# Down-projection of seven of eight feed-forward blocks as seven products of halves

## The chip, the cores and the metric

The kernel runs on one core of one Trainium2 chip. The metric is the device time of one execution in microseconds; lower is better. The core's engines are PE (matmul, with its weight loads listed as PEld), DVE (vector), ACT (scalar), POOL (GpSimd) and SP, which here issues the DMAs. Each engine works through its own queue in order, and semaphores tie the queues together.

## What is computed

One inference step of a two-layer streaming encoder for 1024 prompt frames and 64 sample frames, together T = 1088 columns. The mixing part of a layer (three kinds of attention) isn't touched. The feed-forward part is

```python
D_MODEL = 1024
DEPTH = 2
D_FF = 4 * D_MODEL
...
def _ffn(h, w_up, w_down):
    u = jax.nn.relu(jnp.einsum('bsd,df->bsf', h, w_up))
    return jnp.einsum('bsf,fd->bsd', u * u, w_down)
...
        xp = xp + _ffn(rmsnorm(xp, g_ffn[l]), w_up[l], w_down[l])
        xs = xs + _ffn(rmsnorm(xs, g_ffn[l]), w_up[l], w_down[l])
```

All data are float32. A product is made of three matmuls: each operand is split into a rounded high part and a low remainder (float32r), and high by high, high by low and low by high are summed in PSUM.

## The kernel before

Activations lie transposed, features on the 128 partitions and the T columns in three chunks (`CH`: 384, 384 and 320). The residual `x` is eight tiles of 1088 columns in SBUF. `phase3` runs the feed-forward part of a layer as eight blocks of 512 inner features, one after the other (`ffn_block`, b = 0 to 7).

A block has an up half and a down half. The up half takes four weight tiles (f = 0 to 3) of 128 by 1024: `weight` loads one by DMA, ACT casts it to the high part (L121), DVE subtracts to get the low part (L106). `mm3w` (L977, L979) then makes 8 k-tiles by 3 terms by 3 chunks = 72 matmuls. Each chunk's sum leaves PSUM through `evacuate`: DVE applies relu and the norm factor (L989), ACT squares it into the high part of `U[f]` (L990), POOL squares it in full precision, DVE subtracts the two for the low part.

The down half takes four more weight tiles. Each gives two of the eight output tiles, 4 k-tiles by 3 terms by 3 chunks = 36 matmuls for each, and DVE adds the three PSUM chunks to `x` (L106). So each half has 288 matmuls. There are 8 PSUM buffers (`mm`), 4 buffers for split weights (`wp`), 4 for `U`. The last block (b = 7) runs its last six output tiles chunk by chunk, beside the next layer's norm; this stays as it is.

The order on each engine isn't written out: a scheduler with a time model of its own sets it from the dependencies when the kernel is built.

## Time and profile before

| | us |
|---|---|
| median of 3 runs (lowest to highest) | 2835.04 (2831.56 to 2840.52) |
| the profiled execution's own time | 2833.1 |
| its span | 2831.2 |
| busy of the span: PE, DVE, ACT, POOL | 2748.0, 1458.3, 1066.8, 447.3 |

The span counts from the first to the last instruction of the profiled execution. Busy time on PE is not PE at its peak, since matmuls are pipelined: a record lasts longer than the distance to the next one's start, and it is this distance that counts. The two feed-forward parts are the stretches in which PE is full and DVE, ACT and POOL are low.

### The profile page before, as it was taken

The page shows a single profiled execution, that of the slowest core. Times are in us where ns is not written, and L with a number is a line of the kernel's source. Part 1 is how long each engine was busy: PE and PEld are TensorE (multiplying, and loading weights), DVE is VectorE, ACT ScalarE, POOL GpSimd, SP SyncE. Part 2 cuts the span into 40 slices and gives each one's busy share as a digit, 9 for nine tenths or more (in the row PEclk, how much of TensorE's full clock was granted, in tenths as well). Part 3 has the DMA queues.
Part 4 walks back from the last instruction along what each step waited for, and adds up shares of the span by engine and source line. Part 5 has one row for each costly group of instructions (what it writes and reads, how often), then busy time and mean ns, then how long its engine had stood idle before and what let it go on. Part 6 is the DMA issues. An engine that isn't in the chain of part 4 may idle for free. (4 is left out here: it accounts for less than half of the span.)

```text
span 2831.2 us, 44128 instructions
## 1 busy us (share of the span) xinstructions
PE 2748.0 (97%) x16918; PEld 2651.0 (94%) x16918; DVE 1458.3 (52%) x2968; ACT 1066.8 (38%) x2289; POOL 447.3 (16%) x588
## 2 busy tenths in 40 slices
PE   7999999999999999999999999999999999999997
PEld 6998888899999999999999888888999999999997
DVE  6677676665333333333647786675733333333335
ACT  5666577543111111111437665774521111111113
POOL 1112233201001100110111122431011001101112
PEclk9999999999999999999999999999999999999998
DMA  6657754551111111111265667445311111111111
GB/s 205 203 172 207 237 133 124 158 184 60 41 43 44 46 45 45 46 45 45 75 218 177 190 183 226 139 146 168 129 48 42 44 45 45 45 45 46 45 38 64
DMA packets 211811, 300.34 MB, mean 106 GB/s; under 512 B 34832, under 2 KB 180880, under 8 KB 211600
## 3 DMA queue, kind: packets, MB, share of 16 engines
q1 hardware_dynamic: 211600, 297.51, 34.0%
q8 instruction: 134, 2.20, 0.3%
q14 instruction: 77, 0.63, 0.1%
HBM read 205.72 MB, written 91.72 MB: 105 GB/s over the span
## 5 line engine op out<-in xcount | busy, mean ns | idle before, releaser
L121 ACT CAST w<-wraw 128x1024 fp32r<-128x1024 f32 (+1 forms) x190 | 198.0, 1043 | 1051.2 <-PE mm L979 986.4
L977 PE MATMUL mm<-h,w 128*128 128x384 f32 (+1 forms) x2880 | 550.5, 325 | 0.0
L977 PE MATMUL mm<-u,w 128*128 128x384 f32 (+1 forms) x2784 | 545.0, 328 | 0.0
L977 PEld LDWEIGHTS mm<-h,w 128*128 128x128 f32 x2880 | 500.8, 188 | 0.0
L977 PEld LDWEIGHTS mm<-u,w 128*128 128x128 f32 x2784 | 481.3, 188 | 0.0
L106 DVE TENSOR_TENSOR x<-mm,x 128x384 f32<-128x384 f32 (+1 forms) x432 | 210.3, 530 | 412.2 <-PE mm L979 398.7
L106 POOL TENSOR_TENSOR u<-t 128x384 f32<-128x384 f32 (+1 forms) x192 | 152.0, 791 | 1295.6 <-DVE t L989 1295.6
L979 PE MATMUL mm<-h,w 128*128 128x384 f32 (+1 forms) x1440 | 321.8, 332 | 0.0
L979 PE MATMUL mm<-u,w 128*128 128x384 f32 (+1 forms) x1392 | 311.9, 327 | 0.0
L989 DVE SCALAR_TENSOR_TENSOR t<-mm,r 128x384 f32<-128x384 f32 (+1 forms) x192 | 102.0, 531 | 363.0 <-PE mm L979 362.7
L106 DVE TENSOR_TENSOR w<-wraw,w 128x1024 fp32r<-128x1024 f32 (+2 forms) x244 | 240.1, 1002 | 91.6 <-ACT w L121 90.4
L213 PE MATMUL mm<-h,w 128*128 128x384 f32 (+1 forms) x720 | 242.1, 336 | 15.1 <-ACT w L121 12.3
L979 PEld LDWEIGHTS mm<-h,w 128*128 128x128 f32 x1440 | 241.5, 188 | 0.0
L979 PEld LDWEIGHTS mm<-u,w 128*128 128x128 f32 x1392 | 238.1, 188 | 0.0
L215 PE MATMUL mm<-h,w 128*128 128x384 f32 (+1 forms) x720 | 236.8, 329 | 0.3 <-DVE w L106 0.3
L214 PE MATMUL mm<-h,w 128*128 128x384 f32 (+1 forms) x720 | 236.5, 329 | 0.0
L990 ACT ACTIVATE u<-t 128x384 fp32r<-128x384 f32 (+1 forms) x192 | 97.1, 506 | 204.6 <-DVE t L989 204.6
L106 DVE TENSOR_TENSOR u<-u,u 128x384 fp32r<-128x384 f32 (+1 forms) x192 | 102.5, 534 | 108.6 <-POOL u L106 105.7
L213 PEld LDWEIGHTS mm<-h,w 128*128 128x128 f32 x720 | 136.5, 190 | 18.3 <-ACT w L121 12.3
L214 PEld LDWEIGHTS mm<-h,w 128*128 128x128 f32 x720 | 136.5, 190 | 1.0
L215 PEld LDWEIGHTS mm<-h,w 128*128 128x128 f32 x720 | 136.2, 189 | 0.9 <-DVE w L106 0.8
L758 POOL TENSOR_SCALAR P<-P,mx 128x640 f32<-128x640 f32 (+8 forms) x144 | 101.1, 706 | 208.9 <-DVE mx L757 141.6
(169 smaller groups left out, 4503.0 us busy)
## 6 DMA issues: line engine op xcount, KB each, us to landing
wraw<-in_w_up SPq DMA_DIRECT2D x64, 512.0 KB, 3.6
wraw<-in_w_dn SPq DMA_DIRECT2D x64, 512.0 KB, 3.5
wraw<-in_w_ft SPq DMA_DIRECT2D x24, 512.0 KB, 4.8
Q<-scr_qc SPq DMA_DIRECT2D x64, 128.0 KB, 3.2
Q<-scr_qa SPq DMA_DIRECT2D x64, 128.0 KB, 3.1
qn<-scr_qn SPq DMA_DIRECT2D x32, 256.0 KB, 3.0
Q<-scr_qr SPq DMA_DIRECT2D x64, 128.0 KB, 2.8
scr_qn<-qsp SPq DMA_DIRECT2D x16, 384.0 KB, 3.3
```

The lines of the kernel that those rows point to most:

```text
L106: (eng or self.nc.vector).tensor_tensor(out, a, b, op=op)
L121: self.nc.scalar.copy(w[:, 0], raw)
L213: nc.tensor.matmul(ps, whi(k), rhs(0, k), start=first and k == 0, stop=False)
L214: nc.tensor.matmul(ps, whi(k), rhs(1, k), start=False, stop=False)
L215: nc.tensor.matmul(ps, wlo(k), rhs(0, k), start=False, stop=last and k == nk - 1)
L758: nc.gpsimd.tensor_scalar(P, P, mx[:, 4:5], 0.0, op0=ALU.mult, op1=ALU.add)
L977: nc.tensor.matmul(ps[:, :n], whi(k), rhs(j, k, o, n), start=k == 0 and j == 0, stop=False)
L979: nc.tensor.matmul(ps[:, :n], wlo(k), rhs(0, k, o, n), start=False, stop=k == nk - 1)
L989: nc.vector.scalar_tensor_tensor(t, ps[:, :n], 0.0, rs[c][:, :n], op0=ALU.max, op1=ALU.mult)
L990: nc.scalar.activation(u[:, 0, o:o + n], t, AF.Square)
```

## The change

For blocks 0 to 6 of each layer the down half is made another way (`ffn_down`). The block's weight (512 inner features by 1024 outputs) is four quarters `A11` to `A22`, its activations four quarters `B11` to `B22` (256 features by 544 columns, `HT`). Where the plain way makes eight products of quarters, the new one makes seven products of sums and differences of quarters (Strassen's scheme in Winograd's form). A product is 4 output tiles by 2 k-tiles by 3 terms by 2 column halves of 272 (`QT`) = 48 matmuls, so the down half has 336 matmuls of 272 columns where it had 288 of 384 or 320.

The operands of each product are split anew (`split_w`, `split_u`: a cast on ACT, a subtraction on DVE, 128 by 1024 or 1088). The sums of weights are four 128 by 1024 operations on POOL, in place in the raw tiles `wd`; the sums of activations are four on DVE, in place in `U`, which is now plain float32, written by POOL's square alone. DVE adds every product's PSUM tiles to a quarter of `x` or to a new accumulator `v`. Products 1, 3 and 5 go to a second quarter too: ACT copies the PSUM tile to `tq` and POOL adds it. After block 6, DVE adds `v` to three quarters of `x`. The loads are as many bytes as before, four of 512 KB in each block.

```diff
+HT = T // 2
+QT = T // 4
...
-            up = self.pool(es, "up", 4, side="right")
+            up = self.pool(es, "up", 2, side="right")
-            np = self.pool(es, "np", 1, side="right")
+            wd = self.pool(es, "wd", 4, side="right")
-            for c in range(3):
-                list(self.prep(x, G_FFN + 8 * l, H2, c, np, sh[c]))
+            with ExitStack() as e1:
+                np = self.pool(e1, "np1", 1, side="right")
+                for c in range(3):
+                    list(self.prep(x, G_FFN + 8 * l, H2, c, np, sh[c]))
-            for b in range(7):
-                self.ffn_block(l, b, x, H2, rs, up, tp, mm, late)
+            with ExitStack() as e1:
+                v = self.pool(e1, "v", 1, side="right").tile([128, 4, HT], F32, name="v")
+                tq = self.pool(e1, "tq", 2, side="right")
+                for b in range(7):
+                    U = [up.tile([128, 2, T], F32, name="U", tag="U") for _ in range(2)]
+                    raws = [[wd.tile([128, WSLOT], F32, name="wd", tag="wd") for _ in range(2)] for _ in range(2)]
+                    self.ffn_up(l, b, H2, rs, tp, mm, late, lambda f: U[f // 2][:, f % 2])
+                    self.ffn_down(l, b, x, U, raws, up, mm, v, tq)
+                for d in range(4):
+                    for m, h in ((0, 1), (1, 0), (1, 1)):
+                        xq = x[:, 4 * m + d, HT * h:HT * h + HT]
+                        self.tt(xq, xq, v[:, d], ALU.add)
+            np = self.pool(es, "np", 1, side="right")
             if last:
                 post = lambda: [self.final(x, o, n, mm, np) for o, n in CH]
             else:
                 post = lambda: self.norm_mix(l + 1, x, mm, np, True)
-            self.ffn_block(l, 7, x, H2, rs, up, tp, mm, late, post)
+            U = [up.tile([128, 2, T], F32R, name="u", tag="uU"[f // 2]) for f in range(4)]
+            self.ffn_up(l, 7, H2, rs, tp, mm, late, lambda f: U[f], split=True)
+            self.ffn_last(l, x, U, mm, post)
 
...
-    def ffn_block(self, l, b, x, H, rs, up, tp, mm, late, post=None):
+    def ffn_up(self, l, b, H, rs, tp, mm, late, dst, split=False):
+
         nc, a = self.nc, self.a
-        U, todo = [], []
+        todo = []
 
         def evacuate(u, ps, c):
             o, n = CH[c]
             t = tp.tile([128, CW], F32, name="t", tag="t")[:, :n]
+            nc.vector.scalar_tensor_tensor(t, ps[:, :n], 0.0, rs[c][:, :n], op0=ALU.max, op1=ALU.mult)
+            if not split:
+                self.tt(u[:, o:o + n], t, t, ALU.mult, nc.gpsimd)
+                return
             u2 = tp.tile([128, CW], F32, name="u2", tag="u2")[:, :n]
-            nc.vector.scalar_tensor_tensor(t, ps[:, :n], 0.0, rs[c][:, :n], op0=ALU.max, op1=ALU.mult)
             nc.scalar.activation(u[:, 0, o:o + n], t, AF.Square)
             self.tt(u2, t, t, ALU.mult, nc.gpsimd)
             self.lo(u[:, 1, o:o + n], u2, u[:, 0, o:o + n])
...
-            U.append(up.tile([128, 2, T], F32R, name="u", tag="u"))
...
+    def ffn_down(self, l, b, x, U, raws, up, mm, v, tq):
+
+        nc, a = self.nc, self.a
+        (A11, A12), (A21, A22) = raws
+        for m in range(2):
+            for k in range(2):
+                self.dma(raws[m][k], a["w_dq"][l, b, m, k])
+        B11, B12, B21, B22 = (u[:, :, HT * h:HT * h + HT] for u in U for h in range(2))
+
+        def split_w(src):
+            w = self.wp.tile([128, 2, WSLOT], F32R, name="w", tag="w")
+            nc.scalar.copy(w[:, 0], src)
+            self.lo(w[:, 1], src, w[:, 0])
+            return w.rearrange("p j (k d m) -> p j k d m", k=2, d=4)
+
+        def split_u(src):
+            c = up.tile([128, 2, 2, HT], F32R, name="uc", tag="u")
+            nc.scalar.copy(c[:, 0], src)
+            self.lo(c[:, 1], src, c[:, 0])
+            return c
+
+        def product(w, c, done, also=None):
+
+            for d in range(4):
+                pss = [mm.tile([128, 512], F32, name="mm", tag="mm")[:, :QT] for _ in range(2)]
+                for k in range(2):
+                    for wj, cj in ((0, 0), (0, 1), (1, 0)):
+                        for h in range(2):
+                            nc.tensor.matmul(pss[h], w[:, wj, k, d], c[:, cj, k, QT * h:QT * h + QT],
+                                             start=k == wj == cj == 0, stop=k == wj == 1)
+                if also is not None:
+                    q, new = also(d)
+                    for h in range(2):
+                        qh = q[:, QT * h:QT * h + QT]
+                        t = qh if new else tq.tile([128, QT], F32, name="tq", tag="tq")
+                        nc.scalar.copy(t, pss[h])
+                        if not new:
+                            self.tt(qh, qh, t, ALU.add, nc.gpsimd)
+                for h in range(2):
+                    q = done[:, d, QT * h:QT * h + QT]
+                    self.tt(q, pss[h], q, ALU.add)
+
+        xq = [[x[:, 4 * m:4 * m + 4, HT * t:HT * t + HT] for t in range(2)] for m in range(2)]
+        pool = nc.gpsimd
+        w1, c1 = split_w(A11), split_u(B11)
+        self.tt(A11, A11, A21, ALU.subtract, pool)
+        w2, c2 = split_w(A12), split_u(B21)
+        self.tt(B12, B22, B12, ALU.subtract)
+        self.tt(B11, B12, B11, ALU.add)
+        product(w1, c1, xq[0][0], lambda d: (v[:, d], b == 0))
+        w3, c3 = split_w(A11), split_u(B12)
+        self.tt(A21, A21, A22, ALU.add, pool)
+        self.tt(B21, B21, B11, ALU.subtract)
+        product(w2, c2, xq[0][0])
+        w4, c4 = split_w(A22), split_u(B21)
+        self.tt(A22, A22, A11, ALU.subtract, pool)
+        self.tt(A12, A12, A22, ALU.subtract, pool)
+        self.tt(B12, B22, B11, ALU.subtract)
+        product(w3, c3, xq[1][0], lambda d: (xq[1][1][:, d], False))
+        w5, c5 = split_w(A21), split_u(B12)
+        product(w4, c4, xq[1][0])
+        w6, c6 = split_w(A12), split_u(B22)
+        product(w5, c5, xq[0][1], lambda d: (xq[1][1][:, d], False))
+        w7, c7 = split_w(A22), split_u(B11)
+        product(w6, c6, xq[0][1])
+        product(w7, c7, v)
+
+    def ffn_last(self, l, x, U, mm, post):
+
+        a = self.a
         rhs = lambda j, k, o, n: U[k][:, j, o:o + n]
-        for d2s in ([0], [1], [2], [3]) if b < 7 else ([0], [1, 2, 3]):
-            ws = [self.weight(a["w_dn"][l, b, d2], 8, 128)
-                  for d2 in d2s]
+        for d2s in ([0], [1, 2, 3]):
+            ws = [self.weight(a["w_dn"][l, d2], 8, 128) for d2 in d2s]
             tiles = [(2 * d2 + e, w[0][:, 4 * e:4 * e + 4], w[1][:, 4 * e:4 * e + 4])
                      for d2, w in zip(d2s, ws) for e in range(2)]
...
-    d["w_dn"] = np.ascontiguousarray(
-        f["w_down"].reshape(DEPTH, 8, 4, 128, 4, 2, 128).transpose(0, 1, 4, 3, 5, 2, 6)).reshape(
-            DEPTH, 8, 4, 128, 8, 128)
+    wd = f["w_down"].reshape(DEPTH, 8, 512, 1024)
+    d["w_dn"] = wd[:, 7].reshape(DEPTH, 4, 128, 4, 2, 128).transpose(0, 3, 2, 4, 1, 5).reshape(DEPTH, 4, 128, 8, 128)
+    d["w_dq"] = wd[:, :7].reshape(DEPTH, 7, 2, 2, 128, 2, 4, 128).transpose(0, 1, 5, 2, 4, 3, 6, 7).reshape(
+        DEPTH, 7, 2, 2, 128, 1024)
```

How the queues stand, from the built programs. First DVE, at the change from a block's up half to its down half (blocks 1 and 2 of layer 0). `t` is the relu result, `w` a split weight, `wraw` and `wd` raw weights, `u`, `U` the squared activations, `uc` a split activation operand. Before:

```order
L989 SCALAR_TENSOR_TENSOR t<-mm,r 128x384
L106 TENSOR_TENSOR w<-wraw,w 128x1024
L106 TENSOR_TENSOR u<-u_9128,u 128x384
L989 SCALAR_TENSOR_TENSOR t<-mm,r 128x384
L106 TENSOR_TENSOR u<-u_9134,u 128x384
L989 SCALAR_TENSOR_TENSOR t<-mm,r 128x320
L106 TENSOR_TENSOR x<-mm,x 128x384
L106 TENSOR_TENSOR u<-u_9140,u 128x320
L106 TENSOR_TENSOR x<-mm,x 128x384
L106 TENSOR_TENSOR x<-mm,x 128x320
L106 TENSOR_TENSOR x<-mm,x 128x384 x2
L106 TENSOR_TENSOR x<-mm,x 128x320
```

After:

```order
L1006 SCALAR_TENSOR_TENSOR t<-mm,r 128x384
L108 TENSOR_TENSOR x<-mm,x 128x272 x4
L1006 SCALAR_TENSOR_TENSOR t<-mm,r 128x320
L108 TENSOR_TENSOR w<-wd,w 128x1024
L108 TENSOR_TENSOR uc<-U,uc 128x1088
L108 TENSOR_TENSOR x<-mm,x 128x272 x2
L108 TENSOR_TENSOR U<-U 128x2x544
L108 TENSOR_TENSOR x<-mm,x 128x272 x3
L108 TENSOR_TENSOR U<-U 128x2x544
L108 TENSOR_TENSOR uc<-U,uc 128x1088
L108 TENSOR_TENSOR x<-mm,x 128x272 x3
L108 TENSOR_TENSOR U<-U 128x2x544 x2
```

Between the additions from PSUM there stand now splits and sums of 1024 and 1088 elements. The `w<-wd` behind the last `t` is the split of the fifth weight operand, and the first `uc` behind it is the second product's operand. From the first `x<-mm` here to the seventh product's `uc` DVE's queue has 39 additions from PSUM, 6 `uc`, 4 `U` and 4 `w`.

ACT at the same place, before:

```order
L990 ACTIVATE u<-t 128x320
L121 CAST w<-wraw 128x1024
L990 ACTIVATE u<-t 128x384 x2
L990 ACTIVATE u<-t 128x320
L121 CAST w<-wraw 128x1024 x5
L990 ACTIVATE u<-t 128x384 x2
```

After:

```order
L1046 CAST w<-wd 128x1024 x2
L1070 COPY tq<-mm 128x272 x4
L1046 CAST w<-wd 128x1024
L1052 CAST uc<-U 128x1088
L1070 COPY tq<-mm 128x272 x3
L1052 CAST uc<-U 128x1088
L1070 COPY tq<-mm 128x272
L1046 CAST w<-wd 128x1024
```

ACT has no squares there any more. Its `w<-wd` behind the four copies is the fifth weight operand, and `uc` behind that is the second product's. The fifth weight takes the buffer of the first (four buffers), so ACT waits there for the end of product 1.

POOL, which had only 12 `u<-t` in a block, has these there after the change:

```order
L108 TENSOR_TENSOR U<-t 128x384
L108 TENSOR_TENSOR v<-v,tq 128x272 x2
L108 TENSOR_TENSOR wd<-wd 128x1024
L108 TENSOR_TENSOR U<-t 128x384
L108 TENSOR_TENSOR v<-v,tq 128x272 x2
L108 TENSOR_TENSOR wd<-wd 128x1024
L108 TENSOR_TENSOR U<-t 128x320
L108 TENSOR_TENSOR v<-v,tq 128x272 x4
L108 TENSOR_TENSOR x<-x,tq 128x272 x16
L108 TENSOR_TENSOR U<-t 128x384
```

The squares of the up half's last tile stand between additions to `v` or `x` and sums of weights (`wd<-wd`).

## Rows read from the trace of the kernel before

**Rows 1.** The page: busy of PE; PE's granted clock by slice; the chain's engines.

```profile
PE 2748.0 (97%) x16918; PEld 2651.0 (94%) x16918; DVE 1458.3 (52%) x2968; ACT 1066.8 (38%) x2289; POOL 447.3 (16%) x588
...
PEclk9999999999999999999999999999999999999998
...
PE 28%; DVE 1%; ACT 0%; DVEq 0%; issue 0%; ACTq 0%
```

**Rows 2.** Stretch of one block: us, then busy (count) by engine, clock, DMA.

```profile
932.64:1027.74 95.10, 95.10 (x576) 95.10 (x575) 32.90 (x56) 14.08 (x20) 9.50 (x12) 1.00 0.15 45
```

**Rows 3.** PE in order of time: start, duration, line, operation, shape, count.

```profile
68.79 0.31 PE L213 MATMUL mm<-h,w 128*128 128x320 f32 x1
...
69.96 0.31 PE L215 MATMUL mm<-h,w 128*128 128x320 f32 x1
70.11 8.65 PE L375 MATMUL mm<-w,h 128*128 128x256 f32 x72
78.59 0.34 PE L213 MATMUL mm<-h,w 128*128 128x384 f32 x1
...
79.98 0.33 PE L215 MATMUL mm<-h,w 128*128 128x384 f32 x1
```

**Rows 4.** ACT by shape: count, then busy us, mean ns of one.

```profile
L121 ACT CAST w<-wraw 128x1024 fp32r<-128x1024 f32 x188 | 196.8, 1047 | 1049.4 <-PE mm L979 986.4 <-PE mm L215 34.7 <-DMA wraw<-in_w_uv 6.8
...
L848 ACT COPY vm<-mm 128x256 f32<-128x256 f32 x40 | 14.8, 376 | 5.8 <-PE mm L846 5.3
```

**Rows 5.** DVE in order of time, back to back.

```profile
1049.64 1.23 DVE L106 TENSOR_TENSOR w<-wraw,w 128x1024 fp32r<-128x1024 f32 x1 [0.86 <-ACT w L121]
1050.79 0.55 DVE L106 TENSOR_TENSOR u<-u,u 128x384 fp32r<-128x384 f32 x1
...
2806.33 0.55 DVE L106 TENSOR_TENSOR nsh<-nsh,nsq 128x384 f32<-128x384 f32 x1
2806.80 0.48 DVE L106 TENSOR_TENSOR x<-mm,x 128x320 f32<-128x320 f32 x1
2807.20 0.48 DVE L106 TENSOR_TENSOR nsh<-nsh,nsq 128x320 f32<-128x320 f32 x1
```

**Rows 6.** POOL by shape: one input read twice, then two inputs.

```profile
L106 POOL TENSOR_TENSOR u<-t 128x384 f32<-128x384 f32 x128 | 105.8, 827 | 1215.8 <-DVE t L989 1215.8
...
L106 POOL TENSOR_TENSOR acc<-acc,osq 128x256 f32<-128x256 f32 x24 | 19.2, 801 | 83.7 <-ACT osq L704 83.5
...
L106 POOL TENSOR_TENSOR y<-y 128x384 f32<-128x384 f32 x8 | 8.1, 1008 | 42.5 <-DVE y L784 42.5
```

**Rows 7.** DVE and POOL at once, both on SBUF: near 129 us and 2800 us.

```profile
129.57 1.27 DVE L106 TENSOR_TENSOR lsp<-nh,lsp 128x384 fp32r<-128x384 f32 x1
...
129.41 1.02 POOL L106 TENSOR_TENSOR split<-raw,split 128x384 fp32r<-128x384 f32 x1
...
2800.53 3.96 DVE L947 SCALAR_TENSOR_TENSOR y<-x,gains,r 128x384 f32<-128x384 f32 x3
...
2800.28 3.79 POOL L106 TENSOR_TENSOR y<-y,r 128x384 f32<-128x384 f32 x3 [2.22 <-DVE r L135]
```

**Rows 8.** DVE on PSUM beside POOL on SBUF, at 2810.7 us.

```profile
2810.91 0.49 DVE L106 TENSOR_TENSOR x<-mm,x 128x320 f32<-128x320 f32 x1 [0.87 <-PE mm L215]
...
2810.68 0.88 POOL L106 TENSOR_TENSOR nacc<-nacc,nsq 128x320 f32<-128x320 f32 x1 [6.61 <-ACT nsq L149]
```

**Rows 9.** An idle PE and the stretches behind it (columns as in Rows 2).

```profile
500.90 0.33 PE L662 MATMUL Tp<-cst,P 128*128 128x128 f32 x1 [3.04 <-POOL P L758]
...
500.00:504.00 4.00, 3.10 (x10) 2.16 (x11) 4.00 (x10) 3.88 (x8) 1.82 (x3) 0.67 1.08 372
504.00:508.00 4.00, 4.00 (x26) 3.68 (x25) 3.64 (x9) 3.11 (x10) 1.82 (x3) 0.90 0.78 205
```

More of the change, by code (lines that the diff above doesn't have):

```diff
@@ L1000, in ffn_block @@
                     self.mm3(ps[:, :n], lambda k: hi[:, k], lambda k: lo[:, k], lambda j, k: at(H, j, k, o, n), 8, n)
-                    todo.append((U[f], ps, c))
+                    todo.append((dst(f), ps, c))
                     if (f, c) in ((0, 1), (0, 2), (1, 0)):
@@ L1008, in ffn_block @@
                 self.mm3w(pss, lambda k: hi[:, k], lambda k: lo[:, k], lambda j, k, o, n: at(H, j, k, o, n), 8)
-                todo += [(U[f], ps, c) for c, ps in enumerate(pss)]
+                todo += [(dst(f), ps, c) for c, ps in enumerate(pss)]
                 while todo:
                     evacuate(*todo.pop(0))
+    def ffn_down(self, l, b, x, U, raws, up, mm, v, tq):
[58 more added lines that the diff above has]
+        product(w7, c7, v)
```

## Prediction

> **What bounds the kernel now.** I read the page first, then the windows over one feed-forward block, then single instructions. PE is busy for 97% of the span, its clock is at the upper level (2.4 GHz) in nearly every slice, and the chain that ended last is PE's alone where the page names it [rows 1]. One block, up half and down half, is 576 matmuls in 95.10 us with PE busy all of it, against 32.90 us of DVE, 14.08 of ACT and 9.50 of POOL [rows 2]. So PE bounds the feed-forward part, 16 blocks or 1522 us of the span, and there a matmul taken away is time taken away, as long as PE doesn't begin to wait. The reader is to see both things in rows 2: nothing on PE is free, and the other engines idle for two thirds or more. The change spends that idle time, and spends it in the down half alone.
>
> **What PE saves.** What counts is the distance between starts. Eight 384-column matmuls take 79.98 - 78.59 = 1.39 us, 0.1738 each; eight of 320 columns take 1.17, 0.1463 each; the 72 of 256 columns take 78.59 - 70.11 = 8.48, 0.1178 each [rows 3]. On the line through the last two, 0.00045 us a column, 272 columns cost 0.125 us (0.1248). No row has 272, but it lies close to 256; the ends are 0.1178 and 0.1463. A down half now takes half of 95.10 = 47.55 us. Its successor takes 336 x 0.1248 = 41.93, and one product 48 x 0.1248 = 5.99. That is 5.62 us saved a block, in 14 blocks 78.7 us. If PE never waited, the profiled execution's 2833.1 us would become 2754.
>
> **What the other engines get to do.** Put time 0 at the start of product 1 of a block. DVE's starts lie 0.47 us apart at 384 elements, 0.40 at 320, 1.15 at 1024 [rows 5], so 0.35 at 272 and 1.22 at 1088. Up to the operand `uc` of product 7 its queue has 39 additions from PSUM (13.65 us), 4 weight splits (4.6), 6 `uc` and 4 `U` (12.2) and two relus of the up half (0.87): 31.3 us. It can begin on them when the first output tile is complete and ACT has copied it: 12 matmuls (1.5), 0.17 of drain (a record lasts twice the distance [rows 3]) and about 0.4 for a copy (0.376 at 256 [rows 4]): 2.1. So DVE by itself has product 7 ready at 33.4 us. PE, unhindered, wants it at 6 x 5.99 = 35.9. That is 2.5 us of slack in 36: the cover is there, but only if nothing holds DVE up.
>
> POOL works in the same stretch: 22 of the 24 additions of 272, two sums of weights of 1024 and two squares. Two-input operations cost 0.801 us at 256 and 1.008 at 384 [rows 6], so 0.83 at 272; at 1024 the line through both gives 2.0 and proportion 2.7, and I take 2.3. With the squares (0.83 and 0.72) that is 18.3 + 4.6 + 1.55 = 24.4 us.
>
> **These two get in each other's way.** At 129 us DVE subtracts two SBUF tiles of 384 elements and needs 1.27 us, where the same size takes 0.55 [rows 5]: POOL had begun a 1.02 us operation 0.16 us before, and 129.41 + 1.02 = 130.43, plus DVE's own, is where DVE ends [rows 7]. Near 2800 us three of DVE's operations take 3.96 us and three of POOL's 3.79, both from the same stretch [rows 7]: alone they'd take some 1.5 and 3.0, so they went in turns. With an operand in PSUM DVE isn't held: 0.49 us beside a POOL operation [rows 8]. So DVE's 39 additions from PSUM can run beside POOL, and its 14 operations with two SBUF operands (16.8 us) can't.
>
> The Trainium skill, page "SBUF — State Buffer", section "SBUF: two separate sides", states this as a rule: DVE with two SBUF inputs and GpSimd share one port pair, an exclusive lock held for the whole instruction. The trace agrees by the two stretches just named. By that rule the change would be slower by the sum below, without it faster as in the first rival.
>
> Three values for when product 7's operand is ready:
> - packed at best: POOL has 14.5 us of DVE's PSUM work to run beside, the other 9.9 of its 24.4 us must push DVE back: 33.4 + 9.9 = 43.3, PE waits 7.4;
> - each of the 14 operations waits behind one addition: 33.4 + 14 x 0.83 = 45.0, PE waits 9.1;
> - two of them wait behind a sum of weights instead: 45.0 + 2 x 1.47 = 47.9, PE waits 12.0.
>
> I take 10, between the last two and nearer the middle one, since some find POOL idle.
>
> **Where the wait shows first** is between products 1 and 2. The fifth weight operand takes product 1's buffer and stands in ACT's and DVE's queues ahead of the second product's `uc`. So after product 1's end (0.2 for the drain and the semaphore) come ACT's cast of the fifth weight (1.05 [rows 4]), DVE's subtraction for it (1.15) and DVE's 1.3 for `uc`: 3.7, less the 0.25 of matmuls that need the high part alone: 3.5 us without any contention. Queued behind the waiting subtraction are DVE's remaining additions of product 1, and these hold half of the PSUM buffers. This 3.5 is part of the 10, not on top of it. Once DVE sets the pace, the price of a 272-column matmul matters little: at 0.1463 PE would be slower but DVE ready at the same time.
>
> **The clock.** Behind an idle of 3.04 us PE's granted clock is 0.67 and then 0.90 in two stretches of 4 us [rows 9], so it was at its lower level (1.2 GHz) for some 3.4 us and lost (0.33 + 0.10) x 4 = 1.7 us. The new waits are of that size, one or more in a block. I count 0.9 a block, half, because PE then waits on DVE anyway; the ends are 0 and 1.7.
>
> **What costs nothing, and its cover.** The up half loses ACT's square and DVE's subtraction; they lie beside 47.5 us of PE, so nothing is gained there, but DVE's backlog at a block's end (the last additions and three weight splits) runs off under the next up half, where DVE has some 11 us of work. If that cover failed, 5 to 8 us a block would come on top. The 12 additions of `v` after block 6 (some 0.65 us each, 8 in a layer) lie under the next block's first 72 matmuls, 12 us. The DMA bytes are the same, 45 GB/s in a block [rows 2], and the four loads for block b+1 find their buffers free half a block ahead.
>
> **The sum.** A block: -5.62 + 10 + 0.9 = +5.28 us; 14 blocks: +73.9; 2833.1 + 73.9 = 2907 us. The median of the runs shown lies 1.9 us above the profiled execution, less than I can claim. With 7.4 of waiting and no clock loss it is +1.78 a block, 2858; with 12.0 and 1.7 it is +8.08, 2946.
>
> **Rivals.**
> - *DVE keeps up: faster.* POOL's operations fall beside DVE's PSUM additions, the 2.5 us of slack hold, and only the 3.5 us between products 1 and 2 remain: 14 x (3.5 - 5.62) = -30, 2803; with the clock's 0.9, 2816. For it: POOL waits for ACT's copies, so its work comes in bursts that may miss DVE's. Against it: 24.4 us of POOL work don't fit beside 14.5 us, so it needs the lock seen in rows 7 to hold only sometimes. It decides at 5.6 us of waiting a block. Chance 0.11.
> - *PE never waits* (2754): only if the cast of the fifth weight didn't stand ahead of the second operand, and the order shows that it does. 0.02.
> - *A draw*, 5.0 to 6.2 us of waiting and clock a block: 0.07.
> - *It gets worse*: POOL's 1024-element sums at 2.7 us, or each split waiting for two of POOL's operations; then DVE's additions come so late that PSUM buffers hold PE inside a product as well. 14 us of waiting and 1.7 of clock give +10.1 a block, 2974. Above 2946 I put 0.12.
>
> **How the numbers follow.** The forecast, 2858 to 2946, has 0.62; a milder loss, 2842 to 2858, 0.06. A measurement of this kernel can tell about 0.3% (8.5 us) from no change, so faster is 0.11 + 0.02 = 0.13, the same 0.07, slower 0.80. The range from 2830 to 2962 leaves out most of the faster cases and about half of the worst one, some 0.18 together.
>
> **What would show it.** In the trace after: 48 matmuls of a product that doesn't wait span about 6.0 us (5.6 or 7.0 and the price of 272 columns was off). The down half of a block, from product 1's start to the next up half's, is about 52 to 54 us; at 46 the first rival holds, at 42 the second. PE's idle there is put down to `uc` subtractions on DVE and, between products 1 and 2, to the fifth weight behind it. `w`, `uc` and `U` operations on DVE come out well above 1.23 us in the down half and at 1.23 in the up half, while additions from PSUM stay near 0.43. If they stay at 1.23 everywhere, the contention is not there and the prediction falls. The granted clock is below 1.00 once in each down half. The up halves stay at 47.5 us with no idle.

## The result, and the profile after

The changed kernel takes **2902.1 us** (2899.2 to 2904.1), the kernel before 2835.5 on the same chip: a ratio of 1.0236, 95% interval 1.0222 to 1.0250. The prediction was 2907, slower, with 0.80 on slower. Its profiled execution spans 2900.0 us. From the page, busy time by engine, PE's granted clock by slice, and the chain:

```profile
PE 2729.2 (94%) x17590; PEld 2613.4 (90%) x17590; DVE 1805.9 (62%) x3468; ACT 1245.5 (43%) x2597; POOL 945.5 (33%) x964
...
PEclk9999999999999999999999999999999999999998
...
PE 67%; DVE 11%; issue 7%; DMA 5%; POOL 5%; ACT 4%; SPq 1%; DVEq 0%; POOLq 0%; ACTq 0%
```

Against [rows 1], PE has 19 us less to do in a span 69 us longer, DVE 348 more and POOL 498 more. In the chain DVE has 11% where it had 1%, and POOL and ACT 5% and 4%. Next, stretches as in [rows 2]: one up half, one down half, and the sum of all 14 down halves.

```profile
751.67:799.46 47.79, 47.79 (x291) 47.79 (x290) 11.61 (x17) 5.30 (x5) 11.80 (x11) 1.00 0.04 13
...
1203.37:1255.75 52.38, 45.85 (x339) 44.65 (x338) 44.84 (x74) 21.50 (x37) 34.27 (x29) 0.93 0.23 71
...
sum 734.23, PE 646.43 PEld 630.32 DVE 627.43 ACT 300.73 POOL 461.64; mean PE 46.17 PEld 45.02 DVE 44.82 ACT 21.48 POOL 32.97
```

The up half is what it was, without idle. A down half takes 734.23 / 14 = 52.45 us on average; before it was 47.55, and 14 x 4.9 = 68.6 us is all of the 68.8 between the two spans. So everything happens in the down halves: 41.93 us of matmuls (the prediction's price) and 10.5 us lost. Where in the half they are lost, PE in order of time shows (start, duration, then the idle time before the group and what ended it):

```profile
1203.37 6.15 PE L1063 MATMUL mm<-uc,w 128*128 128x272 f32 x48
1211.65 1.01 PE L1063 MATMUL mm<-uc,w 128*128 128x272 f32 x4 [2.13 <-ACT uc L1052]
1213.99 8.05 PE L1063 MATMUL mm<-uc,w 128*128 128x272 f32 x45 [1.33 <-DVE uc L108]
1223.08 3.17 PE L1063 MATMUL mm<-uc,w 128*128 128x272 f32 x23 [1.04 <-DVE uc L108]
1226.87 3.28 PE L1063 MATMUL mm<-uc,w 128*128 128x272 f32 x24 [0.63 <-DVE x L108]
1231.55 24.36 PE L1063 MATMUL mm<-uc,w 128*128 128x272 f32 x192 [1.40 <-DVE x L108]
```

The first row is one product unhindered: (6.15 - 0.28) / 47 = 0.125 us a matmul (0.28 is the last record's own length), the price taken for 272 columns. Between products 1 and 2 PE idles 2.13 and, after four matmuls that need the high part alone, 1.33: the 3.5 us of the prediction. The last row holds products 4 to 7, and they lose nothing: 192 x 0.125 = 24.0. **In this half all of the loss falls in the first three products**, 28.18 us from 1203.37 to 1231.55 where 144 matmuls need 18.0. In the half that starts at 1101.59 the last wait, 1.41 us for product 4's `uc`, falls on that product's third matmul: 28.6 us for the first 146 matmuls, and 25.4 for the other 190, which need 23.7. These 190 don't wait, but the granted clock is 0.93 in their stretch:

```profile
1130.17:1155.59 25.42, 25.42 (x191) 25.42 (x192) 21.93 (x43) 9.18 (x16) 10.04 (x11) 0.93 0.28 87
```

Such a second fall of the clock, in product 4, stands in five of the fourteen halves; they take 53.5 to 54.1 us. The others take 52.1 to 52.5, apart from the first of each layer (48.9 and 49.4). From product 5 on no half loses anything. What the idle time is put down to, over the whole trace (us, times, longest):

```profile
PE mm L1063 <- DVE uc L108: 38.5, 32, 1.6
PE mm L1063 <- ACT uc L1052: 30.4, 14, 2.4
PE mm L1063 <- DVE x L108: 18.9, 23, 1.9
```

That is 87.8 us, 6.3 a block; the mean clock of the 14 halves (0.91 to 0.97) takes some 3.4 us a block of PE's time more. Next, DVE and POOL by shape (count, then busy us and mean ns of one, then the idle before and what ended it):

```profile
L108 DVE TENSOR_TENSOR uc<-U,uc 128x1088 fp32r<-128x1088 f32 x98 | 149.4, 1524 | 15.6 <-ACT uc L1052 15.6
L108 DVE TENSOR_TENSOR w<-wd,w 128x1024 fp32r<-128x1024 f32 x98 | 130.4, 1330 | 44.4 <-ACT w L1046 44.4
L108 DVE TENSOR_TENSOR U<-U 128x1088 f32<-128x1088 f32 x56 | 82.7, 1485 | 24.9 <-POOL U L108 24.9
...
L108 POOL TENSOR_TENSOR x<-x,tq 128x272 f32<-128x272 f32 x224 | 239.4, 1099 | 167.3 <-ACT tq L1070 167.3
L108 POOL TENSOR_TENSOR wd<-wd 128x1024 f32<-128x1024 f32 x56 | 146.5, 2615 | 20.3 <-DVE w L108 20.3
L108 POOL TENSOR_TENSOR v<-v,tq 128x272 f32<-128x272 f32 x96 | 110.9, 1175 | 9.0 <-ACT tq L1070 7.6
```

DVE's `uc`, `w` and `U` are longer than the 1.22 and 1.15 us of the prediction, but not by 0.83 each; POOL's additions are 1.10 to 1.18 us against the 0.83 forecast. And DVE's sums `U` wait 24.9 us for POOL. Last, rows of DVE in order of time in the half above, the third of them the `uc` of product 4:

```profile
1210.41 0.49 DVE L1006 SCALAR_TENSOR_TENSOR t<-mm,r 128x320 f32<-128x320 f32 x1 [2.27 <-POOL U L108]
...
1216.88 1.83 DVE L108 TENSOR_TENSOR U<-U 128x1088 f32<-128x1088 f32 x1 [2.25 <-POOL U L108]
...
1229.28 1.86 DVE L108 TENSOR_TENSOR uc<-U,uc 128x1088 fp32r<-128x1088 f32 x1
```

Product 4's operand is there at 1231.14, 27.8 us after the half's start, and PE would want it after 3 x 5.99 = 18.0. Of the 27.8 us, DVE stands idle for 4.8 behind its first addition, 4.5 of them for POOL's late squares (the relu result needs the buffer that a square still reads, the sum `U` needs the square). Another 3.0 are `w`, `uc` and `U` operations that last longer than 1.15 and 1.22 us. The remaining 20.0 are its start and its own work, in the order of its queue.

### The profile page after: what moved, and what is told of

It is laid out like the page before. It is cut to its first block, busy times and chain, and to the rows that moved or that the text cites. A ratio compares the mean times of both kernels' runs of the same rounds, so it can differ in the third digit from the quotient of the medians.

```text
span 2900.0 us, 46903 instructions
## 1 busy us (share of the span) xinstructions
PE 2729.2 (94%) x17590; PEld 2613.4 (90%) x17590; DVE 1805.9 (62%) x3468; ACT 1245.5 (43%) x2597; POOL 945.5 (33%) x964
## 4 chain that ended last, share of the span: by engine, by line
PE 67%; DVE 11%; issue 7%; DMA 5%; POOL 5%; ACT 4%; SPq 1%; DVEq 0%; POOLq 0%; ACTq 0%
PE mm L994 17%; PE mm L1063 13%; PE mm L996 9%; PE mm L215 5%; PE mm L217 5%; PE mm L216 5%; PE S L627 4%; PE Tp L664 2%; PE O L680 2%; DVE x L108 2%; PE O L683 2%; POOL wd L108 2%; POOL v L108 2%; DVE uc L108 2%; DVE U L108 1%
## 5 line engine op out<-in xcount | busy, mean ns | idle before, releaser
L1063 PE MATMUL mm<-uc,w 128*128 128x272 f32 x4704 | 648.7, 301 | 87.8 <-DVE uc L108 38.5
L1063 PEld LDWEIGHTS mm<-uc,w 128*128 128x128 f32 x4704 | 631.7, 199 | 103.9 <-DVE uc L108 45.7
L994 PEld LDWEIGHTS mm<-h,w 128*128 128x128 f32 x2880 | 500.4, 188 | 0.0
L108 DVE TENSOR_TENSOR x<-mm,x 128x272 f32<-128x272 f32 (+2 forms) x768 | 304.7, 440 | 43.9 <-ACT tq L1070 18.0
L108 POOL TENSOR_TENSOR U<-t 128x384 f32<-128x384 f32 x168 | 136.7, 814 | 568.1 <-DVE t L1006 568.1
L108 POOL TENSOR_TENSOR x<-x,tq 128x272 f32<-128x272 f32 x224 | 239.4, 1099 | 167.3 <-ACT tq L1070 167.3
L996 PEld LDWEIGHTS mm<-h,w 128*128 128x128 f32 x1440 | 241.5, 188 | 0.0
L123 ACT CAST w<-wraw 128x1024 fp32r<-128x1024 f32 x134 | 139.3, 1040 | 222.9 <-PE mm L1063 105.9
L108 DVE TENSOR_TENSOR w<-wraw,w 128x512 fp32r<-128x512 f32 (+2 forms) x188 | 174.9, 953 | 44.1 <-ACT w L123 43.8
L1070 ACT COPY tq<-mm 128x272 f32<-128x272 f32 x320 | 116.9, 386 | 181.4 <-POOL x L108 79.9
L108 DVE TENSOR_TENSOR uc<-U,uc 128x1088 fp32r<-128x1088 f32 x98 | 149.4, 1524 | 15.6 <-ACT uc L1052 15.6
L108 DVE TENSOR_TENSOR w<-wd,w 128x1024 fp32r<-128x1024 f32 x98 | 130.4, 1330 | 44.4 <-ACT w L1046 44.4
L215 PEld LDWEIGHTS mm<-h,w 128*128 128x128 f32 x720 | 136.0, 189 | 20.6 <-ACT w L123 12.9
```

The costliest lines, as they stand in the source:

```text
L108: (eng or self.nc.vector).tensor_tensor(out, a, b, op=op)
L123: self.nc.scalar.copy(w[:, 0], raw)
L215: nc.tensor.matmul(ps, whi(k), rhs(0, k), start=first and k == 0, stop=False)
L994: nc.tensor.matmul(ps[:, :n], whi(k), rhs(j, k, o, n), start=k == 0 and j == 0, stop=False)
L996: nc.tensor.matmul(ps[:, :n], wlo(k), rhs(0, k, o, n), start=False, stop=k == nk - 1)
L1063: nc.tensor.matmul(pss[h], w[:, wj, k, d], c[:, cj, k, QT * h:QT * h + QT], start=k == wj == cj == 0, stop=k == wj == 1)
```

## The experiments

Each group of runs has its own runs of the kernel before beside it (2831.8 to 2835.5 us), so the runs are compared by their ratio to it. One hundredth of the ratio is 28.35 us, or 2.03 us in each of the 14 blocks. The changed kernel stands at +4.8 us a block. The scheduler ordered DVE's queue anew for each of these kernels, by the traces: only e9 and e11 have it in the same order. A difference between any other two runs holds the new order too.

| run | ratio to before (95%) | us a block |
|---|---|---|
| changed kernel | 1.0236 (1.0222 to 1.0250) | +4.8 |
| e1_no_adds | 1.0023 (1.0013 to 1.0034) | +0.5 |
| e2_adds_dve | 1.0101 (1.0086 to 1.0116) | +2.0 |
| e3_no_wsums | 1.0081 (1.0066 to 1.0096) | +1.6 |
| e4_two_splits | 0.9758 (0.9742 to 0.9774) | -4.9 |
| e7_fill | 1.0218 (1.0200 to 1.0237) | +4.4 |
| e8_act_squares | 1.0125 (1.0108 to 1.0142) | +2.5 |
| e9_no_adds_act_squares | 0.9980 (0.9971 to 0.9990) | -0.4 |
| e10_rebuilt | 0.9901 (0.9884 to 0.9917) | -2.0 |
| e11_no_pool_down | 0.9887 (0.9867 to 0.9906) | -2.3 |
| e12_pool_adds | 1.0008 (0.9999 to 1.0017) | +0.2 |
| e13_sixth_third | 0.9804 (0.9790 to 0.9817) | -4.0 |

**TensorE's term alone.** All products use the operands of the first two:

```diff
-        w3, c3 = split_w(A11), split_u(B12)
...
-        product(w3, c3, xq[1][0], lambda d: (xq[1][1][:, d], False))
+        product(w1, c1, xq[1][0], lambda d: (xq[1][1][:, d], False))
...
```

> Left out: the operands of products 3 to 7 (they use those of products 1 and 2 again), and with them all sums on VectorE and GpSimd; the 336 matmuls, the additions from PSUM, the copies and GpSimd's additions stay. It measures TensorE's term alone. If the 5.62 us a block stand, the down half is 41.9 us at the full clock and the time 2835 - 79 = 2756 us. If draining PSUM (56 additions on VectorE, 24 copies, 24 additions on GpSimd) by itself holds TensorE, it is above 2775.

Measured 2764.2 us, 4.9 us a block under the kernel before. One down half, and POOL's additions there, which now meet few operations of DVE's with two SBUF inputs:

```profile
1154.13:1196.94 42.81, 42.14 (x338) 41.92 (x337) 26.60 (x60) 12.07 (x27) 21.53 (x27) 1.00 0.08 26
...
L108 POOL TENSOR_TENSOR x<-x,tq 128x272 f32<-128x272 f32 x96 | 71.8, 774 | 61.4 <-ACT tq L1070 61.4
```

PE is busy 42.14 us at the full clock, 0.1254 a matmul, and waits 0.67 once, for the second `uc`. The 5.62 us of the prediction are there but for that wait. Draining PSUM doesn't hold PE, and a POOL addition by itself takes 0.774 us, not 1.10.

**Taking work off POOL.** Three runs, each with one edit: the additions left out, the additions on DVE, the sums of weights left out.

```diff
e1:
-                        if not new:
-                            self.tt(qh, qh, t, ALU.add, nc.gpsimd)
e2:
-                        t = qh if new else tq.tile([128, QT], F32, name="tq", tag="tq")
-                        nc.scalar.copy(t, pss[h])
-                        if not new:
-                            self.tt(qh, qh, t, ALU.add, nc.gpsimd)
+                        if new:
+                            nc.scalar.copy(qh, pss[h])
+                        else:
+                            self.tt(qh, pss[h], qh, ALU.add)
e3:
-        self.tt(A11, A11, A21, ALU.subtract, pool)
...
-        self.tt(A21, A21, A22, ALU.add, pool)
...
-        self.tt(A22, A22, A11, ALU.subtract, pool)
-        self.tt(A12, A12, A22, ALU.subtract, pool)
```

> Left out: GpSimd's additions of products 1, 3 and 5 to a second quarter of the result (ScalarE still copies each tile out of PSUM). VectorE's and TensorE's instructions are the same as in the changed kernel. Theory 1 (GpSimd's operations and VectorE's two-SBUF-input operations exclude each other, and GpSimd's queue runs late): a down half falls from 52.45 us to about 46 (41.9 of matmuls, 3.5 between products 1 and 2, 0.5 of clock), so 2902 - 14 x 6.4 = 2812 us; weight sums on GpSimd near 2.3 us; 'uc' near 1.25. Rival (VectorE's own 41 us a down half and the order of its queue set the pace, GpSimd is beside the point): the down half stays above 51, the time above 2880.

> The additions to the second quarter are made by VectorE straight from PSUM, instead of a ScalarE copy and a GpSimd addition. VectorE gets 24 x 0.35 = 8.4 us more in a block, GpSimd loses 26. Theory 1 (exclusion and GpSimd's late queue cost more than the work itself): product 7's operand is ready at 2.1 + 31.3 + 22 x 0.35 = 41.1, TensorE waits 5.2 a block, with 0.9 of clock a down half of 48.0: 2902 - 62 = 2840 us. Rival (VectorE's own load sets the pace): 8.4 us more a block, 2902 + 118 = 3020 us.

> Left out: GpSimd's four sums of weights (products 3, 5, 6 and 7 use the plain quarters). GpSimd loses 4 x 2.6 = 10.5 us of its 33 in a down half. Theory 1: two of the four sums stand ahead of product 7's operand, and a VectorE operation that meets one waits up to 2.6 us: the down half falls by 3 to 4 us, to about 49, 2902 - 49 = 2853 us. Rival (VectorE's own load): 2890 us or more.

Measured 2838.4, 2860.2 and 2855.2 us, beside 2831.8 for the kernel before. Without the additions 4.3 us a block go, and even doing them on DVE, as more work for the engine that is late, saves 2.7. That kills the rival of these runs: it would have had e2 at 3020. The theory's 2812 for e1 and 2840 for e2 were too low. One down half of e1, its PE in order of time, and the sum of 13 down halves of e2:

```profile
1179.88:1227.60 47.72, 44.11 (x338) 43.67 (x337) 42.04 (x74) 21.31 (x37) 7.99 (x5) 0.96 0.25 78
...
1179.88 6.15 PE L1063 MATMUL mm<-uc,w 128*128 128x272 f32 x48
1188.50 1.25 PE L1063 MATMUL mm<-uc,w 128*128 128x272 f32 x8 [2.47 <-ACT uc L1052]
1190.89 36.87 PE L1063 MATMUL mm<-uc,w 128*128 128x272 f32 x280 [1.14 <-DVE uc L108]
```

```profile
sum 647.93, PE 590.54 PEld 580.11 DVE 635.66 ACT 177.58 POOL 103.68; mean PE 45.43 PEld 44.62 DVE 48.90 ACT 13.66 POOL 7.98
```

In e1 the 3.6 us between products 1 and 2 remain, and then PE doesn't wait; its last 280 matmuls take 36.87 us where 280 x 0.125 + 0.3 = 35.3 would do, and the clock is 0.96 in this half. In e2 DVE is busy 48.9 of 49.8 us in a down half: it is full.

All three say less than they seem to, since two things changed at once. In e1 DVE makes two sums `U` and the third product's `uc` soon after the second's:

```profile
1189.03 1.80 DVE L108 TENSOR_TENSOR uc<-U,uc 128x1088 fp32r<-128x1088 f32 x1
1190.76 2.60 DVE L108 TENSOR_TENSOR U<-U 128x1088 f32<-128x1088 f32 x2
...
1193.98 1.28 DVE L108 TENSOR_TENSOR uc<-U,uc 128x1088 fp32r<-128x1088 f32 x1
```

That is 5.0 us from one `uc` to the other; in the changed kernel it is 9.1 (1212.10 to 1221.17). e2 has the two sums at the same place. e3's 3.1 us a block fit the expected 3 to 4, but its trace has no wait of PE for ACT's `uc` any more: with the sums gone the scheduler also put the second `uc` ahead of the fifth weight.

**The clock.** Sixteen matmuls on operands that are ready fill the first idle between products 1 and 2:

```diff
+                for i in range(0 if d else fill):
+                    nc.tensor.matmul(pss[i % 2], w[:, 0, 0, 0], H[0][:, 0, 0, :QT], start=True, stop=True)
...
-        product(w2, c2, xq[0][0])
+        product(w2, c2, xq[0][0], fill=16)
```

> Added: between products 1 and 2 of each of the 14 blocks, 16 matmuls of 272 columns on operands that are ready, into the buffer that product 2 then overwrites (2.0 us, as long as the first wait there, which the changed kernel shows as 2.1 to 2.5 us). They keep TensorE busy in that wait. Theory 'the clock's loss stands beside the waits' (3.5 us a block in the changed kernel): the mean clock of a down half rises from 0.93 to 0.96 or more and the half gets 1.5 to 2 us shorter, 2898 - 14 x 1.75 = 2874 us. Rival (VectorE sets when the next operands are there, and a slower TensorE only waits less): the clock rises, the time stays at 2898 within 8.

Measured 2895.3 us, 1.0218: within what can be told from the changed kernel's 1.0236. One down half:

```profile
1198.36:1250.69 52.33, 47.44 (x354) 45.81 (x353) 43.42 (x74) 21.41 (x37) 34.51 (x29) 0.97 0.21 71
```

The clock rose from 0.93 to 0.97 and the half stayed at 52.3 us. The rival holds where PE has a wait for DVE still ahead: a slower PE only waits less. e9 (below) shows it best. Its fourteen halves take 47.4 us each, five of them at a clock of 1.00 and nine at 0.96. One of each kind:

```profile
796.09:843.49 47.40, 43.70 (x338) 42.42 (x337) 42.83 (x74) 22.05 (x40) 4.81 (x2) 1.00 0.23 78
1081.65:1129.06 47.41, 44.52 (x339) 43.78 (x337) 42.83 (x74) 22.04 (x40) 4.80 (x2) 0.96 0.24 79
```

Behind the last wait it is paid. The five halves of the changed kernel with a fall in product 4 take some 1.6 us more than the others, 0.6 a block on average. In e7 the fall stands in product 4 nowhere, no half takes more than 52.4 us, and the mean of the fourteen is 51.7 in place of 52.45. The two ratios can't tell so little from nothing.

**The order between products 1 and 2.** The last three squares of an up half go to ACT:

```diff
-                self.tt(u[:, o:o + n], t, t, ALU.mult, nc.gpsimd)
+                nc.scalar.activation(u[:, o:o + n], t, AF.Square) if dve else self.tt(u[:, o:o + n], t, t, ALU.mult, nc.gpsimd)
...
-                    evacuate(*todo.pop(0))
+                    evacuate(*todo.pop(0), f == 3)
```

> The last three squares of an up half are made by ScalarE instead of GpSimd. With that the scheduler puts the second product's 'uc' ahead of the fifth weight operand on ScalarE and VectorE; the rest of the down half keeps its work. Theory A (my term of 3.5 us between products 1 and 2 is paid by itself): down half 52.45 - 3.5 or less, 2898 - 49 = 2849 us. Theory B (VectorE and GpSimd set the pace over the whole half, the wait only moves to later products): gain under 1.5 us a block, 2877 us or more.

> Both at once: GpSimd's additions of products 1, 3 and 5 left out, and the last three squares on ScalarE, so the second 'uc' stands ahead of the fifth weight. If the two terms are independent, the 3.5 us and most of the clock's 2 us go from the 47.95 us that a down half takes without the additions: about 43.5, 2838 - 62 = 2776 us. If GpSimd's two sums of weights, which then fall on the second 'uc', hold VectorE by up to 2.4 us, some 2 us remain there: 2805 to 2815 us.

e8 took 2868.5 us, 2.3 us a block less than the changed kernel, between the two theories. The wait for ACT's `uc` is gone, but the one for DVE's additions grew from 18.9 to 51.6 us:

```profile
PE mm L1063 <- DVE x L108: 51.6, 39, 2.4
PE mm L1063 <- DVE uc L108: 17.8, 24, 2.1
```

So about two thirds of the 3.5 us came back, and the rest moved to products 2 and 3. It is no clean price of that wait: the same edit took away DVE's waits for POOL's late squares (24.9 us in front of `U` before, 0.0 in e8). e9 took 2828.2 us, above both of its expected values: fixing the order on top of e1 gave 0.9 us a block. Its trace shows one reason, in three rows (POOL, DVE, PE):

```profile
1179.49 4.89 POOL L108 TENSOR_TENSOR wd<-wd 128x1024 f32<-128x1024 f32 x2 [9.39 <-DVE w L108]
...
1182.28 3.25 DVE L108 TENSOR_TENSOR uc<-U,uc 128x1088 fp32r<-128x1088 f32 x1 [0.68 <-ACT uc L1052]
...
1185.58 14.24 PE L1063 MATMUL mm<-uc,w 128*128 128x272 f32 x96 [2.09 <-DVE uc L108]
```

The second `uc` came early now, met POOL's second sum of weights, and stood until that was through at 1184.38; then it ran its 1.15 us and PE went on at once. This is the exclusion of [rows 7] in its plainest form, 3.25 us for an operation that takes 1.29 alone. These 2 us were in the second expected value. What it lacked is product 4, whose `uc` is late here too: PE gets past it 23.8 us after the half's start, with 148 matmuls done that need 18.5.

**What DVE can do without POOL.** All four sums of weights are made in the up half, the last one out of place, in the up half's raw buffer; with and without the additions:

```diff
         self.tt(A11, A11, A21, ALU.subtract, pool)
+        self.tt(A21, A21, A22, ALU.add, pool)
+        S = self.wr[0].tile([128, WSLOT], F32, name="wraw", tag=self.wr[1])
+        self.tt(S, A22, A11, ALU.subtract, pool)
         w2, c2 = split_w(A12), split_u(B21)
+        self.tt(A12, A12, S, ALU.subtract, pool)
...
-        w7, c7 = split_w(A22), split_u(B11)
+        w7, c7 = split_w(S), split_u(B11)
```

> GpSimd has nothing to do in a down half: its additions of products 1, 3 and 5 are left out, its four sums of weights are made during the up half, the last three squares are on ScalarE. VectorE's work in the down half is that of the changed kernel. By the prediction's sum without contention VectorE has product 7's operand ready at 33.4 us, 2.5 us before TensorE wants it, and the second operand isn't late either: down half near that of the run with two splits (42.8), some 2770 us. Rival: VectorE alone is too slow because of the order of its queue (operands behind additions, PSUM buffers full); TensorE still waits 2 us a block or more: 2795 us or more.

> The same with GpSimd's additions kept: a whole version, the changed kernel with the four sums of weights moved to the up half and the last three squares on ScalarE. Against the run without any GpSimd work in the down half it prices the additions alone. If the additions cost what leaving them out gave before (4.3 us a block), 60 us above it; if most of that price was paid through the late squares and the sums of weights queued behind them, 25 us or less above it.

Measured 2801.2 and 2834.9 us, beside 2833.9. The additions cost 33.7 us, 2.4 a block, once nothing queues behind them, between the two expected values and nearer the lower; the 4.3 of e1 held late squares, sums and a new order as well. What the sums of weights cost, e9 and e11 show: they differ only in where POOL makes these sums, and DVE's order is the same. The second `uc` is now

```profile
1171.36 1.29 DVE L108 TENSOR_TENSOR uc<-U,uc 128x1088 fp32r<-128x1088 f32 x1 [0.68 <-ACT uc L1052]
```

1.29 us where it took 3.25, and the half takes 45.45 us where it took 47.41. Both differ by 1.96: meeting POOL's sum costs this one operation 2.0 us, and the block the same.

But e11 went to its rival: with POOL idle in the down half, PE still waits. PE and DVE in order of time, then DVE by shape:

```profile
1165.92 13.51 PE L1063 MATMUL mm<-uc,w 128*128 128x272 f32 x100
1180.23 6.72 PE L1063 MATMUL mm<-uc,w 128*128 128x272 f32 x48 [0.81 <-DVE uc L108]
1187.76 23.77 PE L1063 MATMUL mm<-uc,w 128*128 128x272 f32 x188 [0.81 <-DVE uc L108]
...
1186.42 1.28 DVE L108 TENSOR_TENSOR uc<-U,uc 128x1088 fp32r<-128x1088 f32 x1
...
L108 DVE TENSOR_TENSOR uc<-U,uc 128x1088 fp32r<-128x1088 f32 x41 | 52.8, 1288 | 10.4 <-ACT uc L1052 10.4
L108 DVE TENSOR_TENSOR w<-wd,w 128x1024 fp32r<-128x1024 f32 x33 | 40.4, 1223 | 16.9 <-ACT w L1046 16.9
...
L108 DVE TENSOR_TENSOR U<-U 128x1088 f32<-128x1088 f32 x24 | 30.8, 1284 | 0.0
```

Every operation of DVE's has its undisturbed length. Product 4's `uc` is ready at 1187.70, 21.8 us after the start, and PE wants it after 3 x 5.99 = 18.0. From there to the end nothing waits (188 matmuls in 23.77 us). So the deadline that DVE misses is that of products 3 and 4: the four sums `U` and three of the splits of weights lie ahead of them.

**A version built on this.** The sums of weights in the up half and the squares on ACT, as above; product 3 into an accumulator of its own, added to both quarters once a layer (8 additions a block fewer); product 5's second additions and half of product 1's on DVE straight from PSUM, the other half of product 1's on POOL. The room comes from one raw buffer in place of two and from `t` taking a pool that is idle there.

```diff
-                v = self.pool(e1, "v", 1, side="right").tile([128, 4, HT], F32, name="v")
-                tq = self.pool(e1, "tq", 2, side="right")
+                vp = self.pool(e1, "v", 2, side="right")
+                v, v3 = (vp.tile([128, 4, HT], F32, name=n, tag="v") for n in ("v", "v3"))
...
-        product(w3, c3, xq[1][0], lambda d: (xq[1][1][:, d], False))
+        product(w3, c3, v3 if b else None, (lambda d: (v3[:, d], True)) if b == 0 else None)
...
+                        elif done is xq[0][0] and h:
...
```

> A whole version built on what the first runs showed: GpSimd's four sums of weights are made during the up half (the last one out of place, in the up half's buffer of raw weights), product 3 goes to an accumulator of its own and is added to both quarters once a layer, product 5's and half of product 1's second additions are made by VectorE from PSUM, the other half of product 1's stay on GpSimd, the last three squares are on ScalarE. VectorE has until product 7's operand about 51 additions (17.9 us), 4 splits of weights (4.6), 10 'uc' and 'U' (12.2), 2 relus (0.9), from 2.1 on: 37.7, 1.8 us after TensorE wants it. Theory (exclusion and order were the cost): down half 42.2 + 0.6 + 2 to 3.5, about 45.5 us, 2898 - 14 x 6.9 = 2801 us, 1% under the kernel before. Rival (VectorE's additions from PSUM come too late and TensorE waits for PSUM buffers): 48 us or more, 2836 us or more, no gain over the kernel before.

Measured **2803.8 us**, 0.9901: below both kernels, as the theory had it. PE in one down half still waits three times, all before product 4 is under way:

```profile
1167.66 12.30 PE L1067 MATMUL mm<-uc,w 128*128 128x272 f32 x97
1180.54 0.74 PE L1067 MATMUL mm<-uc,w 128*128 128x272 f32 x2 [0.58 <-DVE x L108]
1182.08 6.72 PE L1067 MATMUL mm<-uc,w 128*128 128x272 f32 x48 [0.81 <-DVE uc L108]
1189.61 23.97 PE L1067 MATMUL mm<-uc,w 128*128 128x272 f32 x189 [0.81 <-DVE uc L108]
```

That asks for the last edit: product 6, whose operand is a plain quarter of `U`, third.

```diff
-        product(w1, c1, xq[0][0], lambda d: (v[:, d], b == 0))
-        w3, c3 = split_w(A11), split_u(B12)
...
+        product(w1, c1, xq[0][0], lambda d: (v[:, d], b == 0))
+        w6, c6 = split_w(A12), split_u(B22)
+        self.tt(B11, B12, B11, ALU.add)
+        product(w2, c2, xq[0][0])
+        w3, c3 = split_w(A11), split_u(B12)
+        self.tt(B21, B21, B11, ALU.subtract)
+        product(w6, c6, xq[0][1])
```

> The rebuilt version with one edit: product 6, whose operand is a plain quarter, runs third, so that the sums behind products 3, 4 and 5 get 6 us more. All engines keep their work. Theory (the operands of products 3 and 4 are the deadlines that VectorE misses, what comes after is on time): 2 us less a block, 2803.8 - 28 = 2776 us, 2% under the kernel before. Rival (VectorE's load over the whole down half sets the time): 2804 us within 8, as the rebuilt version.

Measured **2777.2 us**, 0.9804, 26.6 less than the rebuilt version where 28 were expected. One down half, and its PE:

```profile
1156.67:1200.43 43.76, 43.21 (x339) 42.38 (x337) 43.43 (x85) 15.27 (x19) 4.88 (x4) 1.00 0.21 67
...
1156.67 14.43 PE L1067 MATMUL mm<-uc,w 128*128 128x272 f32 x114
1171.44 4.03 PE L1067 MATMUL mm<-uc,w 128*128 128x272 f32 x30 [0.34 <-DVE x L108]
1175.68 24.91 PE L1067 MATMUL mm<-uc,w 128*128 128x272 f32 x192 [0.21 <-DVE x L108]
```

The same amount of work, put where its deadline is later, gave 1.9 us a block, so DVE's load over the half was not what held e10. In e13 it nearly is: DVE is busy 43.43 of 43.76 us and PE waits twice for its additions. The first half of each layer, in which DVE is busy 39.9 us and POOL not at all, takes 42.03 us without a wait.

## Why the prediction was right or wrong

- **What bounds, and where.** Right. PE set the pace before, the up halves are untouched, and the loss lies in the down halves alone.
- **What PE saves.** Right: 0.125 us a matmul, and e4 saves 4.9 of the 5.62 us, the rest being one wait of 0.67.
- **The wait between products 1 and 2.** Right in cause and size (2.13 + 1.33 in the block shown). As a price it was too independent: taking the cause away gave 2.3 us a block in e8, where POOL's late squares went with it, and 0.9 in e9, since the next lateness moved up.
- **Contention.** It was there, but its terms were mis-sized. I gave DVE the whole bill, 14 operations of 0.83 us, 11.6 a block. DVE pays, from the means after and those of e11, 7 x 0.107 for `w`, 7 x 0.236 for `uc` and 4 x 0.20 for `U`: 3.2 us. POOL pays, against its times in e4, 16 x 0.325 + 7 x 0.36 for the additions and 4 x 0.21 for the sums against those of e11: 8.6 us (POOL's times in a profile are rough). That the two take turns, and that both pay, stood in [rows 7]; I priced one. What POOL pays comes back to DVE as waiting, since POOL's last squares stand behind sums and additions: 4.5 us ahead of product 4 in the half shown, a term that my sum didn't have. ACT's copy `tq` waits for POOL too (79.9 us behind its additions to `x`, 69.4 behind those to `v`).
- **The deadline: the step that failed.** I made DVE's balance at product 7, where it has 2.5 us of slack without contention, and took that for cover. At product 4, by the same durations, the changed kernel's queue has 16 additions (5.6 us), 3 `uc` and 4 `U` (8.5), 3 splits (3.5) and 2 relus (0.87) from 2.1 on: 20.6, against the 18.0 that PE needs, 2.6 us late before POOL does anything. e11's queue has 20 additions there, 22.0 by the same sum, and its trace shows 21.8. The changed kernel's trace shows 27.8, which is 9.8 late and nearly all of the 10.5 us lost. All the waiting is over with product 4, and the forecast that product 7 would wait for its `uc` was wrong: in the half shown it is there at 43.7 us and PE comes to it at 46.4. That my 10 us came out near was luck. I charged 11.6 us of contention to DVE's operations of nearly the whole half and took 2.5 of slack off it; at product 4 it was 2.0 of DVE's own work, 4.8 of idle and 3.0 of longer operations.
- **The clock.** 0.9 us forecast, 3.4 shown in the records, some 0.6 of it on the path, behind the last wait. That part of it goes under in PE's waits for DVE was forecast and holds.
- **The sum.** 10.9 us of loss a block forecast, 10.5 found; +73.9 us against +66.6. The total was right with a wrong split, by luck, so it would have misled anyone who set out to mend the kernel by it: the first rival's 2803 to 2816 needs, by e11, no POOL work in the down half at all.
- **Signs.** `w`, `uc` and `U` longer in the down half and additions from PSUM at 0.43: as said. Up halves without idle: as said. The clock below 1.00 in each down half: as said, though a second time in five of them. PE's idle put down to `uc` and the fifth weight: as said for 68.9 of the 87.8 us; the other 18.9 wait for DVE's additions, which hold the PSUM buffers, and I had those only in the worst rival.

Not settled: the whole split of the 7.1 us a block between the changed kernel and e11. e9 against e11 puts 2.0 on the sums of weights, by the exclusion alone; e12 against e11 puts 2.4 on the additions, with an order that differs a little. The other 2.7 belong to the late squares and the order together, and no two runs separate these.

## What to carry to other kernels

Make the balance of a supplying engine at every deadline of the engine that it feeds, not only at the last: 2.5 us of slack at the seventh product hid 2.6 us of lateness at the fourth (4 in e11's order), and moving one product that needs no sum to the third place was worth 1% of the kernel. When two engines take turns, price the turn on both, and then ask who waits for the one that you don't watch. Before mending a loss, look for what else is late at the same moment: the terms of the first three products were not independent. Where a scheduler sets the order, compare the queues of two runs before calling their difference the price of what was taken out.

## What the runs showed of the hardware

- DVE with two SBUF inputs and POOL shut each other out for a whole instruction: 3.25 us for a `uc` of 1.29 that met a sum of 2.39, and 1.29 again in e11, where the sum is elsewhere. The Trainium skill, page "SBUF — State Buffer", section "SBUF: two separate sides", states this lock; the three rows of e9 agree with it, to 0.15 us. What I hadn't expected is who pays: POOL's additions went from 0.774 to 1.10 us, 42% up, DVE's operations from 1.29 to 1.52, 18% up.
- DVE's additions with one operand in PSUM took 0.42 to 0.44 us in all of these kernels, with POOL busy 34 us of a down half or none.
- A matmul of 272 columns with its own weights costs 0.125 us at the upper clock, on the line through 256 and 320 columns [rows 3].
